# Prompt attention in a hybrid decoder layer: queries built a unit sooner, compressed scores on column quarters a unit later and transposed in two steps

## The chip, the cores and the metric

The kernel runs on one core of a Trainium2 chip. The metric is the device time of that core for one launch, in microseconds (us). Five engines work side by side, each through its own instructions in the order in which they are written: TensorE (PE; its weight loads are shown apart as PEld), VectorE (DVE), ScalarE (ACT), GpSimd (POOL) and SyncE (SP), which here issues transfers.

## The reference

One step of a decoder layer for 256 prompt tokens and 8 sample sequences of 8 tokens (320 token columns in all): a half FFN, a mixer of two branches (a Mamba-2 scan and a sparse attention with compressed, selected and window parts, 16 query heads on 4 key heads), and a second half FFN.

```python
def rmsnorm(x, g):
    xf = x.astype(jnp.float32)
    y = xf * lax.rsqrt(jnp.mean(xf * xf, axis=-1, keepdims=True) + EPS)
    return (y * g.astype(jnp.float32)).astype(x.dtype)
...
def masked_softmax(s, mask):
    s = jnp.where(mask, s.astype(jnp.float32), -jnp.inf)
    m = jnp.max(s, axis=-1, keepdims=True)
    m = jnp.where(jnp.isfinite(m), m, 0.0)
    e = jnp.exp(s - m)
    return e / jnp.maximum(jnp.sum(e, axis=-1, keepdims=True), 1e-30)
```

The part that the change touches is the prompt's attention. Its compressed branch scores each query against one key for every 32 tokens (8 for 256 tokens), and takes a masked softmax over them. Its values are weighted by these, by the selected and window scores, and by a gate for each head and branch.

## The kernel before

**Dense stream.** All large products (input projection, output projections, both FFNs) run through `dense` (L330 on). For each 128-row group of the contraction it issues three matmuls of 320 columns, which stand for one float32 product: high part by high part (L345), low by high (L346), high by low (L347). I call such three a *k-group*. SP streams the weights in blocks of 512 KB (L308). ACT makes each block's high part (`wh`, L317), and DVE its low part (`wl`, L326), so ACT, then DVE, work ahead of PE on every block.

**Side work.** After each k-group `dense` gives the scheduler a tick (`Sched`, L120 on). The scheduler advances generators, one of which is the attention: every `yield` ends one *step* of it. So a generator's instructions are spread between k-groups, and one step more of waiting moves everything that the generator issues by one step against the dense stream. `wait(n)` is n steps with nothing in them. The same projection feeds the convolution of the Mamba branch: ACT copies (`pr`, L1234), POOL makes the first tap (`cvo`, L1241), DVE three more (L1245), ACT a tanh (`cvt`, L1246), DVE the gated output (L1249, L1252).

**Prompt attention** (`prompt_attn`, L1255 on) has four chunks of 64 queries, eight units each, 32 units in all. POOL clears a buffer (L1267). `build` (L1281) writes a chunk's negated queries into it, in two POOL instructions. `cmp_a` computes the chunk's compressed scores: eight matmuls against 128 columns of queries (L1288), then a chain of small DVE and ACT operations (L1293 to L1303) that makes the softmax and applies the gate. `cmp_b` transposes half of the result on PE (L1310), and ACT copies it (L1311). For each unit there are the scores (PE L1317, DVE L1323, ACT L1326), a norm (DVE L1334, POOL L1337), transposes (PE L1349, ACT copy L1350) and values (PE L1366, with an ACT copy at a chunk's end, L1370).

**Another generator** runs ahead of it: `values_tok` (PE transposes L1035 and L1041, ACT copies), `new_keys` (key transposes, copied by DVE at L1127; PE L1053), and the sample tokens' compressed attention (PE L1212). Behind the attention the Mamba scan reads its states with transfers on SP (`h`, L1770), which stand in SP's one line with the weight blocks; PE uses them at L1819.

**PSUM banks** go by tag, round robin: three for the dense stream, two for `pt`, two for `sc`, one for `po`. A matmul into a bank waits until its last reader is done.

Of the kernel before, what the change touches and what calls it, by code (L numbers as in the profile page):

```python
# [191 lines left out]
def wait(n):  # L192
    for _ in range(n):
        yield
# [3 lines left out]
def step_kernel(ctx, tc, I, O):  # L198
    nc = tc.nc
    pe, v, a, g, sp = nc.tensor, nc.vector, nc.scalar, nc.gpsimd, nc.sync  # L200
# [10 lines left out]
    def bank(tag, shape=(128, 512)):  # L211
        bufs = dict(pd=3, sc=2, pt=2, po=1)[tag]
        t = ps.tile([128, 512], F32, tag=tag, bufs=bufs, name=f"ps_{tag}")[: shape[0], : int(np.prod(shape[1:]))]
        if len(shape) == 3:
            t = t.rearrange("p (a b) -> p a b", a=shape[1])
        elif len(shape) == 4:
            t = t.rearrange("p (a b c) -> p a b c", a=shape[1], b=shape[2])
        return t
# [4 lines left out]
    pt = cp.tile([1, 128], I32, name="pt")  # L223
# [16 lines left out]
    def flat(t):  # L240
        return t.rearrange("p a b -> p (a b)")
# [608 lines left out]
    kTp = pp.tile([128, 2, 8], F32, name="kTp")  # L850
# [17 lines left out]
    def bl(o, m, n):  # L868
        return st["blob"][:, o : o + m * n].rearrange("p (a b) -> p a b", a=m)
# [160 lines left out]

    def values_tok():
        for t in range(2):
            pv = bank("pt")
            for i in range(4):
                pe.transpose(pv[:, 128 * i : 128 * i + 128], vr[:, i, 128 * t : 128 * t + 128], ident)  # L1035
            a.copy(flat(vtp[:, t]), pv)
            yield
        pv = bank("pt", (128, 256))
        for br in range(2):
            for h2 in range(2):  # L1040
                pe.matmul(pv[64 * br : 64 * br + 64, 128 * h2 : 128 * h2 + 128], vr[:, 2 * br + h2, 256:], ident,  # L1041
                          start=True, stop=True)
        a.copy(vst, pv)
        yield
# [216 lines left out]
    def prompt_attn():  # L1261
# [3 lines left out]
        qbp = [bl(1024 * i, 8, 128) for i in range(2)]  # L1265
# [4 lines left out]
        def move():  # L1270
            if ready["prep"] and "OT" not in st:
                st["OT"] = hp_.tile([128, 8, NT], F32, tag="OT", name="OT")
            if moves and "OT" in st:
                t = moves.pop()
                a.copy(st["OT"][:, :, t], qn[:, :, t])


        def build(qc):
            for hp in range(2):
                r = slice(64 * hp, 64 * hp + 64)  # L1280
                g.tensor_scalar(qbp[qc % 2][r, :, 64 * hp : 64 * hp + 64], qn[r, 0:8, 64 * qc : 64 * qc + 64], -1.0, 0.0,  # L1281
                                op0=ALU.mult, op1=ALU.add)

        def cmp_a(qc):
            nb, k0 = 2 * (qc + 1), 192 - 64 * qc
            pc = bank("pt", (128, 8, 8))
            for u in range(8):
                pe.matmul(pc[:, u, :nb], qbp[qc % 2][:, u, :], kTp[:, u // 4, :nb], start=True, stop=True)  # L1288
            sc = pl.tile([128, 8, 8], F32, tag="psc", name="psc")
            m = pl.tile([128, 8], F32, tag="psm", name="psm")  # L1290
            s = sc[:, :, :nb]
            bcast = m.unsqueeze(2).to_broadcast([128, 8, nb])
            v.tensor_tensor(s, pc[:, :, :nb], pb[:, :, k0 + 31 :: 32], op=ALU.add)  # L1293
            v.tensor_reduce(out=m, in_=s, axis=AX.X, op=ALU.min)
            v.tensor_scalar(m, m, 1e20, None, op0=ALU.min)
            v.tensor_tensor(s, s, bcast, op=ALU.subtract)
            a.activation(s, s, AF.Exp, scale=-1.0)
            v.reduce_sum(m, s, axis=AX.X)
            v.tensor_scalar(m, m, 1e-30, None, op0=ALU.max)
            v.reciprocal(m, m)  # L1300
            gq = gtp[:, qc].rearrange("p (u r) -> p u r", r=3)
            v.tensor_tensor(m, m, gq[:, :, 0], op=ALU.mult)
            v.tensor_tensor(s, s, bcast, op=ALU.mult)  # L1303
            pend["c"] = sc

        def cmp_b(qc, q):
            nb, sc = 2 * (qc + 1), pend["c"]
            tps = bank("pt")
            for i in range(4):
                pe.transpose(tps[:nb, 128 * i : 128 * i + 128], sc[:, 4 * q + i, :nb], ident)  # L1310
            a.copy(flat(pcT[qc % 2][:nb, 4 * q : 4 * q + 4]), tps[:nb])  # L1311

        def scores(i):
            qc, u = divmod(i, 8)
            nk, k0 = 64 * (qc + 1), 192 - 64 * qc
            p = bank("sc", (128, 2, 256))
            pe.matmul(p[:, :, :nk], qbp[qc % 2][:, u, :], knp[:, :, u // 4, :nk], start=True, stop=True)  # L1317
            P = pl.tile([128, 2, 256], F32, tag="pS", bufs=4, name="pS")
            if nk % 128:
                g.memset(P[:, :, nk : nk + 64], 0.0)  # L1320
            m = pl.tile([128, 4], F32, tag="pm", bufs=6, name="pm")
            for br in range(2):
                v.tensor_tensor_reduce(out=P[:, br, :nk], in0=p[:, br, :nk], in1=pb[:, u, k0:256], op0=ALU.add,  # L1323
                                       op1=ALU.min, scale=1.0, scalar=3e38, accum_out=m[:, br : br + 1])
            for br in range(2):
                a.activation(P[:, br, :nk], P[:, br, :nk], AF.Exp, bias=m[:, br : br + 1], scale=-1.0,  # L1326
                             accum_out=m[:, 2 + br : 3 + br])
            pend["s", i] = P, m

        def norm(i):  # L1330
            qc, u = divmod(i, 8)
            nk = 64 * (qc + 1)
            P, m = pend["s", i]
            v.reciprocal(m[:, 2:4], m[:, 2:4])  # L1334
            for br in range(2):
                o = 3 * u + 1 + br
                g.tensor_scalar(P[:, br, :nk], P[:, br, :nk], m[:, 2 + br : 3 + br], gtp[:, qc, o : o + 1], op0=ALU.mult,  # L1337
                                op1=ALU.mult)


        def transposes(i):
            nt = (i // 8 + 2) // 2
            P = pend.pop(("s", i))[0]
            tps = bank("pt")
            pT = pl.tile([128, 4, 128], F32, tag="pT", bufs=2, name="pT")
            for k in range(nt):
                for br in range(2):
                    o = (k * 2 + br) * 128
                    pe.transpose(tps[:, o : o + 128], P[:, br, 128 * k : 128 * k + 128], ident)  # L1349
            a.copy(flat(pT[:, 0 : 2 * nt, :]), tps[:, 0 : 256 * nt])  # L1350
            pend["t", i] = pT

        def values(i):

            qc, u = divmod(i, 8)
            h2, nt = u // 4, (qc + 2) // 2
            pT = pend.pop(("t", i))
            if u == 0:
                pend["po"] = bank("po", (128, 8, 64))
            po = pend["po"]  # L1360
            parts = [(vtp[:, k, br, 128 * h2 : 128 * h2 + 128], pT[:, 2 * k + br]) for k in range(nt) for br in range(2)]
            parts.append((flat(vcp[:, 2 * h2 : 2 * h2 + 2, :]), pcT[qc % 2][:, u]))
            for j, (w, x_) in enumerate(parts):
                for hp in range(2):
                    h = slice(64 * hp, 64 * hp + 64)
                    pe.matmul(po[h, u, :], w[:, h], x_[:, h], start=j == 0, stop=j == len(parts) - 1)  # L1366
            if u == 7:

                o = st["OT"] if "OT" in st else qn
                a.copy(o[:, :, 64 * qc : 64 * qc + 64], po)  # L1370
                if o is qn:
                    moves.append(slice(64 * qc, 64 * qc + 64))

        build(0)
        yield from wait(2)
        cmp_a(0)
        yield from wait(4)
        cmp_b(0, 0)
        cmp_b(0, 1)
        for i in range(4):  # L1380
# [6 lines left out]
        for i in range(32):  # L1387
            qc, u = divmod(i, 8)
            if i + 3 < 32:
                norm(i + 3)  # L1390
            if i + 1 < 32:
                transposes(i + 1)
            if i + 4 < 32:
                scores(i + 4)
            yield
            values(i)
            move()
            if qc < 3:
                if u == 1:
                    build(qc + 1)  # L1400
                elif u == 2:
                    cmp_a(qc + 1)
                elif u == 4:
                    cmp_b(qc + 1, 0)
                    cmp_b(qc + 1, 1)
            yield
        pr_stack.close()
        yield from until("prep")
# [467 lines left out]
    def attention():  # L1876
        yield from chain(pace(3), prompt_attn(), pace(4), ssd(), pace(5), sample_attn(), pace(6), merge_prep())
# [54 lines left out]
    for i in range(4):  # L1932
# [5 lines left out]
        c, h2 = divmod(i, 2)  # L1938
# [281 lines left out]
```

## Time and profile before

| what | value |
|---|---|
| runs | 1324.02, 1332.32, 1332.83 us (median 1332.32) |
| profiled execution | 1327.57 us, of which the trace spans 1325.9 us |
| busy share of the span | PE 95%, PEld 87%, DVE 66%, ACT 45%, POOL 28% |
| mean granted clock of TensorE | 0.982 of full speed |

The trace is of one execution, and 1.67 us of its time lie outside the span. A busy share is an average over stages with different limits. The attention of the prompt lies between about 498 and 659 us of the span.

### The profile page before, as it was taken

The page shows a single profiled execution, that of the slowest core. Times are in us where ns is not written, and L with a number is a line of the kernel's source. Part 1 is how long each engine was busy: PE and PEld are TensorE (multiplying, and loading weights), DVE is VectorE, ACT ScalarE, POOL GpSimd, SP SyncE. Part 2 cuts the span into 40 slices and gives each one's busy share as a digit, 9 for nine tenths or more (in the row PEclk, how much of TensorE's full clock was granted, in tenths as well). Part 3 has the DMA queues.
Part 4 walks back from the last instruction along what each step waited for, and adds up shares of the span by engine and source line. Part 5 has one row for each costly group of instructions (what it writes and reads, how often), then busy time and mean ns, then how long its engine had stood idle before and what let it go on. Part 6 is the DMA issues. An engine that isn't in the chain of part 4 may idle for free.

```text
span 1325.9 us, 28576 instructions
## 1 busy us (share of the span) xinstructions
PE 1262.7 (95%) x10779; PEld 1149.6 (87%) x10779; DVE 877.8 (66%) x1872; ACT 590.7 (45%) x1149; POOL 372.7 (28%) x625
## 2 busy tenths in 40 slices
PE   8999999999999998889998898998989999999998
PEld 8899999999988888777896576776769999999998
DVE  5576666655576577975578687778667766666542
ACT  4344444454444334446664343456563343333322
POOL 2232321323100335655435353444420010000000
PEclk9899999999989999999999899999999999999999
DMA  8466665677653445511177775899973534444553
GB/s 278 153 210 216 209 200 190 219 227 216 212 163 125 142 138 206 191 66 63 49 223 244 220 222 174 315 357 313 343 274 115 178 130 146 156 146 157 152 162 92
DMA packets 98501, 251.67 MB, mean 190 GB/s; under 512 B 14649, under 2 KB 41274, under 8 KB 96410
## 3 DMA queue, kind: packets, MB, share of 16 engines
q1 hardware_dynamic: 81370, 198.24, 45.5%
q0 software_dynamic: 16992, 51.61, 11.7%
q8 instruction: 85, 1.39, 0.4%
q14 instruction: 54, 0.43, 0.1%
HBM read 235.07 MB, written 23.10 MB: 195 GB/s over the span
## 4 chain that ended last, share of the span: by engine, by line
PE 57%; DVE 17%; issue 12%; ACT 5%; DMA 4%; POOL 3%; SPq 1%; POOLq 1%; DVEq 0%; ACTq 0%
PE ps_pd L345 15%; PE ps_pd L346 13%; PE ps_pd L347 13%; DVE wl L326 4%; ACT wh L317 2%; DVE cvo L1245 2%; DMA out_ssmS<-h 2%; PE ps_sc L1478 2%; PE ps_po L1518 1%; PE ps_sc L713 1%; PE ps_sc L714 1%; PE ps_sc L723 1%; PE ps_pt L1504 1%; PE ps_po L1366 1%; PE ps_sc L1317 1%
## 5 line engine op out<-in xcount | busy, mean ns | idle before, releaser
L345 PE MATMUL ps_pd<-hh,wh 128*128 128x320 f32 x1320 | 440.7, 334 | 2.9 <-ACT hh L261 1.8
L326 DVE TENSOR_TENSOR wl<-wraw,wh 128x1024 fp32r<-128x1024 f32 (+1 forms) x245 | 305.4, 1248 | 184.9 <-ACT wh L317 179.4
L346 PE MATMUL ps_pd<-hl,wh 128*128 128x320 f32 x1320 | 413.4, 313 | 1.3 <-DVE hl L454 1.1
L347 PE MATMUL ps_pd<-hh,wl 128*128 128x320 f32 x1320 | 413.5, 313 | 1.1 <-DVE wl L326 1.1
L317 ACT CAST wh<-wraw 128x1024 fp32r<-128x1024 f32 (+1 forms) x245 | 252.2, 1031 | 139.8 <-PE ps_pd L346 100.7
L345 PEld LDWEIGHTS ps_pd<-hh,wh 128*128 128x128 f32 x1320 | 252.9, 192 | 22.0 <-issue 11.3
L346 PEld LDWEIGHTS ps_pd<-hl,wh 128*128 128x128 f32 x1320 | 253.4, 192 | 9.6 <-issue 4.8
L347 PEld LDWEIGHTS ps_pd<-hh,wl 128*128 128x128 f32 x1320 | 252.6, 191 | 1.6 <-DVE wl L326 1.6
L345 PE MATMUL ps_pd<-ah,wh 128*128 128x320 f32 x352 | 109.4, 311 | 0.0
L347 PE MATMUL ps_pd<-ah,wl 128*128 128x320 f32 x352 | 108.9, 309 | 0.0
L580 DVE TENSOR_TENSOR pgl<-pg,pgh 128x512 fp32r<-128x512 f32 x128 | 82.5, 685 | 29.7 <-ACT pgh L573 28.8
L346 PE MATMUL ps_pd<-al,wh 128*128 128x320 f32 x320 | 98.8, 309 | 0.0
L568 POOL DMA_DIRECT2D pg<-in_cache x136 | 74.2, 546 | 83.4 <-DVE pgl L580 42.3
L238 POOL TENSOR_SCALAR ah<-ff 128x320 fp32r<-128x320 f32 x44 | 20.1, 456 | 272.5 <-DVE ff L482 272.5
L573 ACT CAST pgh<-pg 128x512 fp32r<-128x512 f32 x128 | 72.7, 617 | 9.7 <-PE ps_sc L714 9.0
L477 ACT ACTIVATE sg<-sg 128x320 f32<-128x320 f32 x44 | 20.8, 472 | 125.7 <-DVE sg L476 125.7
L1431 POOL DMA_DIRECT2D KV<-in_cache x102 | 54.9, 539 | 76.4 <-PE ps_po L1518 43.2
L713 PE MATMUL ps_sc<-pgh,w1h 128*128 128x256 f32 x256 | 68.5, 288 | 1.0 <-ACT pgh L573 1.0
L714 PE MATMUL ps_sc<-pgh,w1l 128*128 128x256 f32 x256 | 68.3, 289 | 0.0
L345 PEld LDWEIGHTS ps_pd<-ah,wh 128*128 128x128 f32 x352 | 66.2, 188 | 0.4
L347 PEld LDWEIGHTS ps_pd<-ah,wl 128*128 128x128 f32 x352 | 66.1, 188 | 0.0
L346 PEld LDWEIGHTS ps_pd<-al,wh 128*128 128x128 f32 x320 | 60.2, 188 | 0.0
(476 smaller groups left out, 2207.9 us busy)
## 6 DMA issues: line engine op xcount, KB each, us to landing
wraw<-in_wproj SPq DMA_DIRECT2D x77, 512.0 KB
KV<-in_cache POOLq DMA_DIRECT2D x102, 256.0 KB, 6.1
wraw<-in_w1in SPq DMA_DIRECT2D x44, 512.0 KB
wraw<-in_w2in SPq DMA_DIRECT2D x44, 512.0 KB
pg<-in_cache POOLq DMA_DIRECT2D x136, 128.0 KB, 4.0
pg<-in_cache SPq DMA_DIRECT2D x120, 128.0 KB
wraw<-in_w1out SPq DMA_DIRECT2D x16, 512.0 KB
h<-in_ssm SPq DMA_DIRECT2D x32, 256.0 KB
```

The lines of the kernel that those rows point to most:

```text
L317: a.copy(h[:, :n], st["raw"][i][:, :n])
L326: v.tensor_tensor(l[:, :n], st["raw"].pop(i)[:, :n], st["hl"][i][0][:, :n], op=ALU.subtract)
L345: pe.matmul(out, wh[:, s], xh[:, kk, :], start=kk == 0, stop=False)
L346: pe.matmul(out, wh[:, s], xl[:, kk, :], start=False, stop=False)
L347: pe.matmul(out, wl[:, s], xh[:, kk, :], start=False, stop=kk == K - 1)
L568: e.dma_start(page(s, half)[:, i, :], I["cache"][ds(r, 1), :, 256 * c : 256 * c + 256].rearrange("o p f -> p (o f)"))
L573: a.copy(h[:, 8 * half : 8 * half + 8, :], page(s, half)[:, :, 64 * q : 64 * q + 64])
L580: v.tensor_tensor(l[:, 8 * half : 8 * half + 8, :], page(s, half)[:, :, 64 * q : 64 * q + 64], h[:, 8 * half : 8 * half + 8, :], op=ALU.su ...
L713: pe.matmul(ph, wh[:, j, :], h[:, :, j, :], start=q + j == 0, stop=False)
L714: pe.matmul(ph, wl[:, j, :], h[:, :, j, :], start=False, stop=False)
L1245: v.scalar_tensor_tensor(o, pr[:, k : k + 344], w(k), o, op0=ALU.mult, op1=ALU.add)
L1431: e.dma_start(t[:, j, :], I["cache"][ds(r, 1), :, 512:1024].rearrange("o p f -> p (o f)"))
```

## The change

There are four edits. First, the second of two banks in `values_tok` comes from the tag `sc` instead of `pt`. Second, each compressed-score matmul against 128 columns of queries becomes four, against 32 columns each, and each writes 32 output rows: 32 instructions for a chunk instead of 8. Third, at the start the wait ahead of the first `cmp_a` is four steps instead of two, and the one behind it three instead of four: seven steps instead of six before the first unit. Fourth, in the loop over units `build` of the next chunk comes at unit 0 (was 1), `cmp_a` at unit 3 (was 2), and the two halves of `cmp_b` at units 5 and 6 (were both at 4).

```diff
     def values_tok():
         for t in range(2):
-            pv = bank("pt")
+            pv = bank("sc" if t else "pt")
...
             for u in range(8):
-                pe.matmul(pc[:, u, :nb], qbp[qc % 2][:, u, :], kTp[:, u // 4, :nb], start=True, stop=True)
+                for c in range(4):
+                    o = slice(32 * c, 32 * c + 32)
+                    pe.matmul(pc[o, u, :nb], qbp[qc % 2][:, u, o], kTp[:, u // 4, :nb], start=True, stop=True)
...
         build(0)
-        yield from wait(2)
+        yield from wait(4)
         cmp_a(0)
-        yield from wait(4)
+        yield from wait(3)
         cmp_b(0, 0)
         cmp_b(0, 1)
...
             if qc < 3:
-                if u == 1:
+                if u == 0:
                     build(qc + 1)
-                elif u == 2:
+                elif u == 3:
                     cmp_a(qc + 1)
-                elif u == 4:
-                    cmp_b(qc + 1, 0)
-                    cmp_b(qc + 1, 1)
+                elif u in (5, 6):
+                    cmp_b(qc + 1, u - 5)
             yield
```

On PE, the compressed scores of the last chunk (`blob` is the queries' buffer, `pT` and `vtp` the transposed weights and the values), before:

```order
L1366 MATMUL ps_po<-pT,vtp 64x64 x8
L1366 MATMUL ps_po<-blob,vcp 64x64 x2
L1288 MATMUL ps_pt<-kTp,blob 128x8 x8
L345 MATMUL ps_pd<-hh,wh 128x320
L346 MATMUL ps_pd<-hl,wh 128x320
L347 MATMUL ps_pd<-hh,wl 128x320
L1349 MATMUL ps_pt<-con,pS 128x128 x4
```

and after:

```order
L1368 MATMUL ps_po<-pT,vtp 64x64 x8
L1368 MATMUL ps_po<-blob,vcp 64x64 x2
L1290 MATMUL ps_pt<-kTp,blob 32x8 x32
L345 MATMUL ps_pd<-hh,wh 128x320
L346 MATMUL ps_pd<-hl,wh 128x320
L347 MATMUL ps_pd<-hh,wl 128x320
L1351 MATMUL ps_pt<-con,pS 128x128 x4
```

The neighbours are the same, and 32 matmuls of 32 rows stand where 8 of 128 stood. Counted in k-groups from the start of the program, the four chunks' `cmp_a` stand behind the 738th, 775th, 818th and 845th before, and the 743rd, 783rd, 826th and 849th now; the scan starts behind the 883rd before and the 884th now.

On POOL, the queries of the second chunk (L1281; `pr`, `ncv` and `cvo` are the convolution's, `pS` the scores being normed), before:

```order
L238 TENSOR_SCALAR pr_4944<-scv 128x8x3
L238 TENSOR_SCALAR ncv<-pr_4944 128x3
L238 TENSOR_SCALAR ncv<-pr_4944 128x24
L1241 TENSOR_SCALAR cvo<-pr_4944,cwh 128x344
L1281 TENSOR_SCALAR blob<-qn 64x8x64 x2
L1337 TENSOR_SCALAR pS<-pS,pm,gtp 128x64 x2
L1320 MEMSET pS 128x2x64
```

and after:

```order
L1322 MEMSET pS 128x2x64
L1281 TENSOR_SCALAR blob<-qn 64x8x64 x2
L238 TENSOR_SCALAR pr_4944<-scv 128x8x3
L238 TENSOR_SCALAR ncv<-pr_4944 128x3
L238 TENSOR_SCALAR ncv<-pr_4944 128x24
L1241 TENSOR_SCALAR cvo<-pr_4944,cwh 128x344
L1339 TENSOR_SCALAR pS<-pS,pm,gtp 128x64 x2
```

The two instructions that write the queries have moved ahead of one convolution unit.

On SP, the scan's state loads (`h`), before:

```order
L1625 DMA abs<-ascr 64x8x64
L1625 DMA ab<-ascr 128x8x128
L1770 DMA h_8768<-in_ssm 128x512
L1770 DMA h_8775<-in_ssm 128x512
L1723 DMA out_ssmS<-h_8299 128x512
L308 DMA wraw<-in_wproj 128x1024
L1770 DMA h_8793<-in_ssm 128x512
```

and after:

```order
L1626 DMA abs<-ascr 64x8x64
L1626 DMA ab<-ascr 128x8x128
L308 DMA wraw<-in_wproj 128x1024
L1771 DMA h_8874<-in_ssm 128x512
L1771 DMA h_8881<-in_ssm 128x512
L1724 DMA out_ssmS<-h_8402 128x512
L1771 DMA h_8895<-in_ssm 128x512
```

One weight block (L308) now stands ahead of two state loads that it stood behind. The same happens in one other batch of the scan's loads, and in one later batch the other way round.

## Rows read from the trace of the kernel before

**Rows 1.** The head of the page, and the busy time of each engine with its share of the span.

```profile
span 1325.9 us, 28576 instructions
PE 1262.7 (95%) x10779; PEld 1149.6 (87%) x10779; DVE 877.8 (66%) x1872; ACT 590.7 (45%) x1149; POOL 372.7 (28%) x625
```

**Rows 2.** Windows: a stretch of the span (us), its length, the busy time and count of PE, PEld, DVE, ACT and POOL, the granted clock, the share of the DMA engines and their GB/s.

```profile
486.90:571.00 84.10, 67.89 (x704) 61.40 (x701) 69.40 (x178) 37.13 (x115) 51.96 (x90) 0.94 0.50 183
...
600.00:626.00 26.00, 25.98 (x263) 21.48 (x262) 16.60 (x64) 18.12 (x55) 14.83 (x34) 1.00 0.13 42
```

**Rows 3.** The chain of waits from 480 to 640 us: start (us), length (us), the engine, tile and line on the chain.

```profile
497.98 3.46 POOL blob L1267
...
502.27 0.79 POOL blob L1281
503.10 1.96 PE ps_pt L1288 x16
...
507.20 1.14 DVE wl L326
...
551.22 0.50 ACT cvt L1246
...
583.65 1.89 PE ps_pt L1288 x16
...
616.55 1.88 PE ps_pt L1288 x16
```

**Rows 4.** Waits of DVE, ACT and POOL from 486.9 to 571 us, by what they waited for: total us, times, longest. The first row is the only one of the three engines' lists in which PE is waited for.

```profile
DVE psc L1293 <- PE ps_pt L1288: 0.5, 1, 0.5
...
DVE wl L326 <- ACT wh L317: 6.9, 6, 1.6
...
ACT cvt L1246 <- DVE cvo L1245: 22.7, 6, 5.7
...
POOL ncv L238 <- ACT pr L1234: 12.1, 7, 4.8
```

**Rows 5.** Waits of PE from 486.9 to 626 us, in the same columns.

```profile
PE ps_po L1366 <- ACT qn L1370: 3.6, 1, 3.6
PE ps_pt L1288 <- POOL blob L1281: 2.9, 2, 2.0
PE ps_pt L1310 <- ACT pT L1350: 2.9, 1, 2.9
PE ps_pt L1035 <- DVE kTp L1127: 2.6, 1, 2.6
...
PE ps_pt L1349 <- ACT blob L1311: 0.7, 1, 0.7
```

**Rows 6.** The timeline of the four compressed-score groups: start, length (us), engine, line, operation, tiles, shapes, count of passes (two for each float32 matmul), and the idle time before with what ended it.

```profile
503.10 1.95 PE L1288 MATMUL ps_pt<-kTp,blob 128*128 128x2 f32 x16 [0.88 <-POOL blob L1281]
...
537.88 1.95 PE L1288 MATMUL ps_pt<-kTp,blob 128*128 128x4 f32 x16 [2.03 <-POOL blob L1281]
...
583.58 1.95 PE L1288 MATMUL ps_pt<-kTp,blob 128*128 128x6 f32 x16
...
616.48 1.95 PE L1288 MATMUL ps_pt<-kTp,blob 128*128 128x8 f32 x16
```

**Rows 7.** The timeline of two other groups of 64 small passes, against 32 columns of weights (L1212, which also fills four quarters of output rows in turn) and against 64 columns (L1053).

```profile
593.15 1.10 PE L1212 MATMUL ps_sc<-kcv,cpT 128*32 128x64 f32 x64
...
496.91 2.04 PE L1053 MATMUL ps_sc<-ksm,qbs 128*64 128x8 f32 x64
```

**Rows 8.** Windows of 3.4 us, PE alone: stretch, length, busy time and count, granted clock, DMA share, GB/s.

```profile
494.20:497.60 3.40, 3.40 (x36) 0.72 0.38 145
...
504.40:507.80 3.40, 3.40 (x22) 0.79 0.04 7
507.80:511.20 3.40, 3.40 (x19) 0.71 0.86 328
541.80:545.20 3.40, 3.40 (x26) 0.69 0.02 5
...
585.40:588.80 3.40, 3.40 (x27) 1.00 0.00 0
```

**Rows 9.** The timeline around the second bank of `values_tok`: the copy that frees it, its transposes, and the next user of the tag.

```profile
491.18 0.16 DVE L1127 COPY kTp<-ps_pt 128x16 f32<-128x16 f32 x1
491.40 0.66 PE L1035 MATMUL ps_pt<-con,vr 128*128 128x128 f32 x4 [2.58 <-DVE kTp L1127]
492.97 1.13 PE L1041 MATMUL ps_pt<-con,vr 128*64 128x128 f32 x8
```

**Rows 10.** The timeline behind the first compressed scores: ACT's high part and DVE's low part of the block in work, and one score operation of a unit on DVE from further on.

```profile
504.26 1.06 ACT L317 CAST wh<-wraw 128x1024 fp32r<-128x1024 f32 x1
507.12 1.22 DVE L326 TENSOR_TENSOR wl<-wraw,wh 128x1024 fp32r<-128x1024 f32 x1
...
532.84 0.20 DVE L1323 CUSTOM_DVE_ANT_0 pS<-ps_sc,pb 128x64 f32<-128x64 f32 x1
```

**Rows 11.** The timeline of the second chunk's queries on POOL.

```profile
535.66 2.17 POOL L1281 TENSOR_SCALAR blob<-qn 64x512 f32<-64x512 f32 x2
```

**Rows 12.** PE's waits for the scan's states from 680 to 1000 us, and a window of that stage (columns as in rows 2).

```profile
PE ps_po L1819 <- DMA h<-in_ssm: 8.9, 5, 2.9
...
720.00:760.00 40.00, 34.54 (x203) 24.47 (x200) 26.57 (x43) 12.39 (x27) 18.37 (x14) 0.87 0.68 216
```

## The prediction

> **What bounds the kernel now.** I read the head of the page first: PE is busy for 1262.7 of 1325.9 us [rows 1]. That is an average, so I next read windows over the prompt's attention, where the edits lie. It falls into two stages [rows 2]. From 486.9 to 571 us PE is busy for 67.89 of 84.10 us and DVE for 69.40. In a stage behind it, 600 to 626 us, PE is busy for 25.98 of 26.00 us, and no other engine is near that.
>
> The chain of waits says who sets the pace in each [rows 3]. In the first stage its pieces are POOL's clearing of the buffer, POOL's queries, DVE's low parts and ACT's tanh; of the edited lines only the first compressed scores (1.96 us at 503.10) are on it on PE's side. At 537.88, where the second chunk's scores ran [rows 6], the chain is elsewhere. In the second stage the third and the fourth chunk's scores are on it (1.89 us at 583.65, 1.88 us at 616.55).
>
> The waits say the same from the other side. Between 486.9 and 571 us DVE waited for PE once, for 0.5 us; ACT and POOL never did [rows 4]. Their long waits are for each other: ACT's tanh for DVE's convolution, 22.7 us; POOL's `ncv` for ACT's copy, 12.1 us; DVE's low part for ACT's high part, 6.9 us. That loop (copy, first tap, three taps, tanh, and on the way the split of the next block) paces the stage. PE's own waits there [rows 5] are then mostly the time that it has to spare: a wait removed comes back as a wait for the next low part.
>
> **The change part by part.**
>
> *Column quarters.* Before, a chunk's scores are 16 passes in 1.95 us [rows 6]; now they are 64 passes of a quarter of the columns. The nearest row has the same form, 64 passes against 32 columns, four quarters of output rows in turn: 1.10 us. The other end is 64 passes against 64 columns, 2.04 us [rows 7]. So a group becomes 0.85 us shorter (1.95 - 1.10) or, at the other end, 0.09 us longer; the four together give 3.4 us back, or cost 0.4. I take 0.85, as the row of 1.10 us has the same column count and the same turn of output rows. Only the third and the fourth chunk lie where PE sets the end, so 2 x 0.85 = **1.7 us** are on the path (the bounds are 3.4 saved and 0.4 lost).
>
> Those 64 passes at L1212 took 17 ns each (1.10 us by 64) [rows 7]. [...]
>
> *The first compressed scores, two steps later.* They left a wait of 0.88 us for POOL's queries and 1.95 us of work [rows 6], on the chain [rows 3]. Behind them the low part started at 507.12, though ACT's high part had ended at 505.32 (504.26 + 1.06) [rows 10]; DVE did the softmax chain of that chunk in between. Now the low part, and the convolution's taps, stand ahead of that chain. So up to 1.8 us could go, but the chain's operations come behind the taps all the same, on an engine with 69.40 us of work in 84.10. Between 0 and 1.8 I take **0.5 us**, near the lower end since only the order of DVE's work changes.
>
> *Queries sooner, scores later, in the loop.* The waits of PE for POOL's queries (2.9 us in two) should go, and those at the transposes in two steps with them (2.9 and 0.7 us) [rows 5], as three units instead of one now lie between writing and use, and one copy of ACT instead of two behind each transposed half. The 2.03 us at the second chunk are off the chain, and so are the transposes' 2.9 us, behind which the chain stands at ACT's tanh (551.22) [rows 3]. I cost both at **nothing**: DVE's work is their cover, and were it gone, 2.0 + 2.9 + 0.7 = 5.6 us would be the gain. What is late next is the low part of the next block. The two POOL instructions (2.17 us) [rows 11] now stand ahead of a convolution unit's first tap. POOL has 12.1 us of waiting for ACT's copies in this stage [rows 4], in seven waits, mean 1.7 us, and that hides them; if one fell on a late copy, up to 2.2 us would be lost. I take nothing.
>
> *The second bank of `values_tok`.* The wait of 2.58 us for the key copy goes to the next user of the tag, the transposes at L1041, which now wait for the same copy (it ends at 491.34) [rows 9]. Of 2.58 us some 1.6 can go: that next group started 1.57 us behind the waiting one (492.97 - 491.40), and it can at most come so much sooner. At 491 us the chain is on POOL and DVE, and POOL's buffer clearing (497.98) [rows 3] is not behind PE. I take **nothing** (bounds 0 and 1.6 saved).
>
> *The clock.* [...] One fall covers two windows, at 0.79 and 0.71, and takes 3.4 x (0.21 + 0.29) = 1.7 us of work from them. [...]
>
> *One step more at the start.* The attention's operations move one step against the dense stream, which takes about four DVE operations of a unit at 0.20 us each [rows 10], **0.8 us**, out of the stage that DVE paces into the one where DVE has time. The bounds are 0 and 2, and the other way 0.5 lost where the tail behind the attention comes later. In the scan, one weight block moves ahead of state loads in two batches and behind in one; costed at nothing, since PE's waits for the states, 8.9 us in five [rows 12], may grow or shrink with it. This is the second rival.
>
> The sum is 1.7 + 0.5 + 0.8 = 3.0 us less. Against the profiled execution's 1327.57 us that is 1324.6. This execution is 4.75 us below the median shown (1332.32); the four executions, this one and the three runs, average 1329.2. As the forecast is compared with runs and not with this execution, I put it at 1329.2 - 3.0, rounded: **1326 us**.
>
> **The rivals.**
>
> *All of PE's gains reach the end.* Then the quarters give 3.4, the queries' waits 2.9, the transposes' 2.9 + 0.7, `values_tok` 1.6 and the clock 5.1: 16.6 us, so 1327.6 - 16.6 = **1311 us**. For it speaks that PE is busy for 95% of the span and that a shorter wait on PE frees weight buffers sooner. Against it speak the chain and that nobody waited for PE [rows 3, 4]. Chance 0.13.
>
> *The states come late.* Where a 512 KB block goes ahead of the states, they land later by its passage: at 216 GB/s [rows 12] 2.4 us, in two batches 4.8. Each such stall of PE can draw a stretch at a lower clock as in [rows 8], 1.7 us each, 3.4 together. Slower by 8.2 us, **1336 us**. It decides once PE's waits for the states exceed the 8.9 us of now by more than the 3.0 us won. Against it: a later batch moves the other way round, and the weight block that now goes first is itself one that the dense stream needs. Chance 0.12.
>
> *The quarters save nothing*, or weight loads don't overlap: 2.04 us for a group instead of 1.95, all four on the path, 0.4 us lost, and the rest a wash: **1328 to 1330 us**, no change. It decides if a small pass lasts as at L1053 (2.04 us by 64, 32 ns) and not as at L1212. [...] Chance 0.10.
>
> **How the numbers follow.** The forecast has the remaining 0.65. About 1%, 13 us, is what a measurement of this kernel can tell from no change. The forecast's own range goes from 3.4 + 1.8 + 2 = 7.2 us saved to 0.4 + 2.2 + 0.5 = 3.1 lost, on a base of 1324.6 to 1332 that the runs spread over: 1319 to 1335. For 8 in 10 the range also goes three quarters of the way from 1324.6 to the first rival, and takes in the second: **1314 to 1337 us**. Faster by over 1% is the first rival nearly whole, 0.11; slower by over 1% needs the second rival and a loss at POOL together, 0.06; within 1% stays 0.83.
>
> **What would show it.** In the profile of the changed kernel: four groups of 64 passes at 1.1 us in place of 1.95; no wait of PE for POOL's queries at any chunk; the wait at the transposes below 1 us; and, between 487 and 571 us, waits of PE for the low part in place of those that went, with this stage's length within 2 us of 84.1. The third and the fourth chunk's scores should still be on the chain, shorter. The forecast is wrong if that stage becomes shorter by much of what PE no longer waits (then the first rival holds), or if the waits for the states exceed 12 us (then the second).

## The result, and the profile after

The change made the kernel slower. Its median is 1337.03 us over 14 runs (1333.65 to 1343.95), against 1331.51 us for the kernel before in the same comparison. The recorded ratio of the two is 1.0064, with a 95% interval of 1.0048 to 1.0080. That is 8.5 us, less than the 1% that I had named as telling apart, but clear of this measurement's noise. The two medians alone differ by 5.5 us (1.0041), so the size is less sure than the sign. The forecast of 1326 us had the sign wrong, and the range ended at 1337.

The head of the page of the changed kernel, answering to [rows 1]:

```profile
span 1337.8 us, 28951 instructions
PE 1266.5 (95%) x10971; PEld 1151.7 (86%) x10971; DVE 878.0 (66%) x1872; ACT 589.4 (44%) x1149; POOL 373.9 (28%) x625
```

The work is the same: DVE, ACT and POOL are busy for as long as before, within 1.3 us, and the span is 11.9 us longer. That is more than the change costs by its runs: the traced execution of the changed kernel (1339.42 us) lies above its median, that of before (1327.57 us) below. So the question is where PE waits or runs slowly. To find the place I followed one operation that every weight block has, DVE's low part (L326), and read its start in both traces at the same block. First the kernel before, at the 131st and the 141st block, then the changed kernel at the same two:

```profile
774.10 1.21 DVE L326 TENSOR_TENSOR wl<-wraw,wh 128x1024 fp32r<-128x1024 f32 x1
...
849.19 1.22 DVE L326 TENSOR_TENSOR wl<-wraw,wh 128x1024 fp32r<-128x1024 f32 x1
```

```profile
770.16 1.21 DVE L326 TENSOR_TENSOR wl<-wraw,wh 128x1024 fp32r<-128x1024 f32 x1
...
855.22 1.22 DVE L326 TENSOR_TENSOR wl<-wraw,wh 128x1024 fp32r<-128x1024 f32 x1
```

Up to the first of them the changed kernel is 3.9 us ahead. (At the 90th block, ahead of all edits, the traces of the seventeen kernels of this document stand up to 8 us apart. So only lengths of stretches are compared here.) Over the next ten blocks, all in the Mamba scan, it falls 10.0 us back (85.06 us where 75.09 were needed), and 3 us are lost in each of two stretches further on; what loses these is not shown. The attention, which the edits are about, is not where the time went: between the starts of the 96th and the 121st block (498.00 to 690.27 us before, 496.55 to 685.50 us after) it is 3.3 us shorter.

PE's waits of the changed kernel between 480 and 660 us, answering to [rows 5]:

```profile
PE ps_pt L1351 <- POOL pS L1339: 7.1, 3, 6.3
PE ps_pt L1312 <- DVE psc L1305: 4.9, 1, 4.9
PE ps_pt L1351 <- ACT pT L1352: 3.3, 1, 3.3
PE ps_pt L1312 <- ACT blob L1313: 2.4, 2, 1.8
...
PE ps_pt L1041 <- DVE kTp L1127: 1.3, 1, 1.3
```

The waits for POOL's queries are gone, and others have taken their place: 4.9 us for DVE's softmax of the first chunk, 7.1 us for the norm. The quarters themselves did more than forecast. Here are the timeline of the first group and the weight loads of all four, in place of the 1.95 us and 128 columns of [rows 6]; the other three groups took 0.71 to 0.72 us:

```profile
501.48 0.85 PE L1290 MATMUL ps_pt<-kTp,blob 128*32 128x2 f32 x64
...
L1290 PEld LDWEIGHTS ps_pt<-kTp,blob x256: 106/110/113, 501.5 to 620.0; 128*32 128x32 f32 x128
```

PE's waits of the changed kernel from 760 to 900 us:

```profile
PE ps_pt L1848 <- DVE ys L1836: 6.6, 1, 6.6
PE ps_sc L1825 <- DVE h L1827: 2.9, 3, 2.2
PE ps_po L1820 <- DMA h<-in_ssm: 2.1, 1, 2.1
```

The first row is new. It is the transpose of `ys`, the part of the sample tokens' output that comes from their states. What it waits for is read from two timelines and the chain of waits. SP's timeline, the kernel before and then the changed one:

```profile
820.13 6.70 SPq L1723 DMA_DIRECT2D out_ssmS<-h  x4
826.88 0.42 SPq L1723 DMA_DIRECT2D out_ssmP<-St  x1
829.76 1.62 SPq L1431 DMA_DIRECT2D KV<-in_cache  x2
831.87 0.34 SPq L308 DMA_DIRECT2D wraw<-in_wproj  x1
```

```profile
818.86 6.66 SPq L1724 DMA_DIRECT2D out_ssmS<-h  x4
830.91 0.34 SPq L308 DMA_DIRECT2D wraw<-in_wproj  x1
831.30 0.42 SPq L1724 DMA_DIRECT2D out_ssmP<-St  x1
```

POOL's, the kernel before and then the changed one (`[...]` is the idle time before a row, and what ended it):

```profile
822.96 2.07 POOL L1821 TENSOR_TENSOR h<-h,cdb 128x512 f32<-128x512 f32 x2 [6.09 <-issue]
830.25 1.16 POOL L1431 DMA_DIRECT2D KV<-in_cache  x2 [5.21 <-DVE zth L2002]
831.42 2.36 POOL L1821 TENSOR_TENSOR h<-h,cdb 128x512 f32<-128x512 f32 x2
```

```profile
823.37 2.09 POOL L1822 TENSOR_TENSOR h<-h,cdb 128x512 f32<-128x512 f32 x2 [7.53 <-DMA out_ssmS<-h]
836.15 1.16 POOL L1432 DMA_DIRECT2D KV<-in_cache  x2 [10.70 <-DMA out_ssmP<-St]
837.33 2.08 POOL L1822 TENSOR_TENSOR h<-h,cdb 128x512 f32<-128x512 f32 x2
```

And the chain of waits of the changed kernel through the same stretch (start, length, what):

```profile
829.67 1.23 DVE wl L326
830.91 0.34 SPq L308
...
831.30 4.16 DMA out_ssmP<-St
...
838.34 1.07 POOL h L1822
839.44 0.69 DVE h L1827
840.12 0.60 DVE ys L1836
...
841.57 1.22 DVE wl L326
```

Read from the top: the weight block's load (L308) waits until DVE has used up a buffer: it goes at 830.91 us, where the low part ends (829.67 + 1.23). In the changed order it stands in SP's line ahead of the last store of the prompt's state (`out_ssmP`). The data of the store were ready at 821.37 us (DVE, L1711), and nothing else stood ahead on SP from 825.52 us on. But the store waits with the block until 831.30 instead of going at 826.88. POOL's next instruction, a load of the sample attention's keys (`KV`), waits for that store (the program closes the pool that holds the stored tile just ahead of these loads). Behind it on POOL stands the scaling of the states, `h`, which DVE needs for `ys`, which PE needs. PE stands still for 6.65 us.

The low parts of the 137th and the 138th block enclose this wait: they start at 829.67 and 841.57 us here, and at 830.63 and 835.95 before. So 6.6 of the 10.0 us arise in this one place. The other 3 build up ahead of it; kernels with SP's order of before, further down, are up to 3.0 us longer there too.

### The profile page after: what moved, and what is told of

Read it like the earlier page. It is cut to its first block, busy times and chain, and to the rows that moved or that the text cites. A ratio compares the mean times of both kernels' runs of the same rounds, so it can differ in the third digit from the quotient of the medians.

```text
span 1337.8 us, 28951 instructions
## 1 busy us (share of the span) xinstructions
PE 1266.5 (95%) x10971; PEld 1151.7 (86%) x10971; DVE 878.0 (66%) x1872; ACT 589.4 (44%) x1149; POOL 373.9 (28%) x625
## 5 line engine op out<-in xcount | busy, mean ns | idle before, releaser
L326 DVE TENSOR_TENSOR wl<-wraw,wh 128x1024 fp32r<-128x1024 f32 (+1 forms) x245 | 304.5, 1244 | 184.8 <-ACT wh L317 180.4
```

The lines of the kernel that those rows point to most:

```text
L326: v.tensor_tensor(l[:, :n], st["raw"].pop(i)[:, :n], st["hl"][i][0][:, :n], op=ALU.subtract)
```

## The experiments

Theory Q: the one step more at the start moves the scan against the dense stream, weight blocks come to stand ahead of the scan's transfers on SP, and the scan pays. The rivals: the edits inside the attention cost it (A); it is the granted clock, falling at places that no order decides (C). Every ratio below is to the kernel before, timed together with it; the bracket is its 95% interval, and a number of us is the ratio's distance from 1 times the median of before.

**The step alone, and the change without it.**

```diff
-        yield from wait(4)
+        yield from wait(5)
         cmp_b(0, 0)
```

> The kernel before with one thing changed: the second wait at the start of the prompt attention is 5 steps instead of 4, seven in all, as in the change; no quarters, no moved build, scores or transposes. Its order on SP is that of the change. Theory Q (the one step puts weight blocks ahead of stores and state loads in SP's line, and the scan pays for it): slower than before by 8 to 14 us, ratio 1.006 to 1.010, with a wait of PE of 4 us or more at the transposes of ys (L1847). Rival A (the edits inside the attention cost the time, for instance by falls of the clock): no difference from before, ratio 0.998 to 1.002. Rival C (falls of the granted clock at places that no order decides): anything between 0.998 and 1.008, with no long wait behind the last store of the prompt's state.

Measured: 1.0134 [1.0105, 1.0163], 17.8 us slower, more than expected. Its one new long wait from 760 to 900 us:

```profile
PE ps_pt L1847 <- DVE ys L1835: 6.2, 1, 6.2
```

```diff
         cmp_a(0)
-        yield from wait(3)
+        yield from wait(2)
```

> The change with the second wait at the start 2 steps instead of 3, six in all, as before; all else of the change kept. Its order on SP is that of the kernel before. Theory Q: faster than before by the attention's gain alone, 2 to 5 us, ratio 0.996 to 0.999, and no wait of PE over 2 us at the transposes of ys. Rival A: as slow as the change, ratio 1.004 to 1.008. Rival C: between 0.997 and 1.008.

Measured: 0.9977 [0.9951, 1.0004], 3.1 us faster or no difference. The step alone makes a worse kernel than the whole change, and the change without the step loses nothing: rival A falls, and C with it, as the same fall would have to follow the step in one kernel after the other. The two do not add up, though: 17.8 less 3.1 would be 14.7 us, and the change measured 8.5. What makes up the difference stays open. In the attention of the kernel without the step PE waits longer for DVE's softmax than in the change (9.5 us in two, where there are 4.9 in one), without harm:

```profile
PE ps_pt L1312 <- DVE psc L1305: 5.7, 1, 5.7
PE ps_pt L1351 <- DVE psc L1295: 3.8, 1, 3.8
```

**Which of the two that the step moves, attention or scan.**

```diff
             yield
+        yield
         pr_stack.close()
```

> The kernel before with one empty step behind the last unit of the prompt attention, so that the attention itself stands as before and the scan one step later; the order on SP is that of the change. Theory Q (the scan's place in the dense stream costs the time): nearly the whole cost of the step at the start, slower than before by 10 to 18 us, ratio 1.008 to 1.014, with a wait of PE of 4 us or more at the transposes of ys. Rival A2 (most of that cost is the later attention): 0 to 5 us, ratio 1.000 to 1.004.

Measured: 1.0107 [1.0082, 1.0132], 14.2 us slower, with the same wait, of 6.8 us:

```profile
PE ps_pt L1848 <- DVE ys L1836: 6.8, 1, 6.8
```

The counterpart has seven steps at the start and leaves out the last empty step behind the units:

```diff
-        yield from wait(4)
+        yield from wait(5)
...
-            yield
+            if i < 31:
+                yield
         pr_stack.close()
```

> The kernel before with seven steps at the start of the attention, and the empty step behind its last unit left out: the attention stands one step later, the scan where it stood; the order on SP is that of the kernel before. Theory Q: within 3 us of before, ratio 0.998 to 1.002. Rival A2: slower by 8 us or more, ratio above 1.006.

Measured: 1.0033 [1.0014, 1.0051], 4.4 us slower. The two parts, 14.2 and 4.4, come to 18.6, close to the 17.8 of the step at the start. So the scan carries most of it, and the attention's later place a part that neither theory had expected. From the 101st to the 111th block that part shows (stretch, length, busy time and count of PE, PEld, DVE, ACT, POOL, granted clock, DMA), the kernel before and then this one:

```profile
535.71:624.45 88.74, 76.92 (x719) 66.35 (x714) 67.98 (x201) 45.68 (x144) 54.00 (x103) 0.96 0.27 96
```

```profile
534.64:628.30 93.66, 83.09 (x740) 71.41 (x740) 68.27 (x201) 46.64 (x149) 51.26 (x106) 0.89 0.26 91
```

The stretch is 4.9 us longer at the same work, and the granted clock is 0.89 where it was 0.96; PE is busy for 6 us more. Whether the clock or the waits around it come first wasn't tried.

The same cut on the change, its scan put back and its attention left a step later:

```diff
-            yield
+            if i < 31:
+                yield
         pr_stack.close()
```

> The change in full, with the empty step behind the attention's last unit left out, so that the scan stands where it stood before; the order on SP is that of the kernel before. Theory Q: as the change without its extra step, faster than before by 2 to 5 us, ratio 0.996 to 0.999. Rival A2: still slower than before, ratio above 1.003.

Measured: 1.0019 [1.0001, 1.0038], 2.5 us slower, between the two expectations. By the middle values two thirds of the change's loss (6.0 of 8.5 us) are gone with the scan's place alone, and against the 0.9977 with six steps the attention's later place costs 0.4% here too. The traces place a part of that: from the 101st to the 106th block the four kernels with the attention of the change (this one, the change itself and two more below) need 45.9 to 46.1 us, and the four with its moves in the loop and six steps 42.8. In every trace the order on SP is as expected: the step alone and the step behind have the order of the change, and the kernel without the step, the one with seven steps and this one have that of before.

**Is it SP's order, or the later place on PE and DVE?** SP's order can be put back without moving the scan: the loads of 28 weight blocks are issued behind the fifth k-group of a block instead of the third.

```diff
             st["hl"][i][1] = l
-            w_load()
+            if not 122 <= i < 150:
+                w_load()
...
+                if k == 4 and 122 <= st["split"] - 1 < 150:
+                    w_load()
                 if (kk + 1) % cut == 0:
```

> The change, with the loads of 28 weight blocks of the scan's stage (numbers 122 to 149) issued behind the fifth k-group of the block in work instead of the third. So SP's order is again that of the kernel before, but for two blocks that stand one or two places later still; on PE, DVE, ACT and POOL the scan keeps the change's later place. Theory Q (SP's order is what the later scan pays for): 6 to 9 us of the change's loss come back, ratio to before 0.999 to 1.002, no wait of 4 us at the transposes of ys. Rival P (the later place of the scan's operations on PE and DVE is what costs): as the change, 1.005 to 1.008.

Measured: 0.9987 [0.9969, 1.0005]. The whole loss came back, with the scan as late as in the change. By the middle values that is more than the scan's share: the attention stands late here too, and its 0.4% is not seen in this kernel. On SP the store now goes right behind the stores of the states:

```profile
816.91 0.33 SPq L1727 DMA_DIRECT2D out_ssmS<-h  x1
817.30 0.70 SPq L1727 DMA_DIRECT2D out_ssmP<-St  x1
820.20 0.91 SPq L1435 DMA_DIRECT2D KV<-in_cache  x2
```

and `ys` is not among PE's waits from 760 to 900 us, which begin with:

```profile
PE ps_pt L399 <- DVE ncol L404: 3.3, 1, 3.3
PE ps_sc L1828 <- DVE h L1830: 2.9, 3, 2.2
PE ps_po L1823 <- DMA h<-in_ssm: 1.7, 1, 1.7
```

Two more kernels ask whether the later loads are a gain of their own. The same edit on the kernel before:

> The kernel before with nothing but the 28 weight loads of the scan's stage behind the fifth k-group instead of the third; the scan stands where it stood, so that SP's order is now a new one, in which weight blocks stand behind transfers of the scan that they stood ahead of. If the later loads are a gain by themselves, and the change's recovery came from that: ratio 0.990 to 0.995. Theory Q (what counts is where the blocks stand among the scan's transfers): no such gain, 0.998 to 1.012.

Measured: 0.9986 [0.9968, 1.0004], no gain that can be told. And the same edit with the empty step behind the last unit:

> The kernel before with the empty step behind the last unit (which alone gave a ratio of 1.0107) and the 28 loads behind the fifth k-group. Theory Q in its barest form: SP's order is back but for two blocks, so the loss goes, ratio 0.997 to 1.002, and no wait of PE of 4 us at the transposes of ys. Rival P (the later place on PE and DVE costs): above 1.006.

Measured: 0.9982 [0.9960, 1.0003], against 1.0107 with the step alone. Between these two kernels only the place of the weight loads differs, and it is worth 1.2%. Theory Q stands for the scan, and the scan's later place on PE and DVE costs nothing that can be told. The traces say the same: between the 137th and the 138th block the change, the step alone and the step behind lose 6.6, 6.6 and 6.7 us against the kernel before, and no other kernel of this document more than 0.9.

**That one store, or several transfers.** The change, with the last store one step sooner:

```diff
                     load_ecb(q + 1)
+                if i == 7:
+                    store("outS")
                 yield
                 store("outS")
```

> The change, with the last store of the prompt's state (out_ssmP) issued one step sooner, so that it stands ahead of the weight block that the change had put in front of it; nothing else moves on SP. Theory Q in its narrow form (that one store behind that one weight block holds POOL's KV loads, the scaling of the states behind them on POOL, and so PE at the transposes of ys): 6 to 9 us of the loss come back, ratio to before 0.999 to 1.002. Theory Q in its wide form (several transfers moved, each costs a part): 1 to 4 us come back, ratio 1.003 to 1.005. Rival A and rival C: as the change, 1.005 to 1.008.

Measured: 1.0029 [1.0009, 1.0048]; by the middle values 4.7 of 8.5 us came back, between the narrow and the wide form. As 2.5 us stayed lost with the scan's place put back altogether, that is most of the scan's share. In the trace the stretch from the 131st to the 141st block is 8.6 us shorter than in the change. The store now goes out ahead of two stores of states, and the wait at `ys` is gone:

```profile
818.13 0.33 SPq L1724 DMA_DIRECT2D out_ssmP<-St  x1
818.52 4.31 SPq L1724 DMA_DIRECT2D out_ssmS<-h  x2
```

The other way round, the kernel before with that store one step later, behind a weight block and two stores of states:

```diff
                 yield
+                if i == 7:
+                    yield
                 store("outS")
```

> The kernel before, with one more step of waiting ahead of the last store of the prompt's state, so that a weight block and two stores of states stand in front of it, as one block does in the change; everything up to that point is as before. Narrow form of theory Q: slower than before by 5 to 9 us, ratio 1.004 to 1.007, with a wait of PE of 4 us or more at the transposes of ys. Wide form: 0 to 3 us, ratio 1.000 to 1.002. Rivals A and C: no difference, 0.998 to 1.002.

Measured: 1.0049 [1.0022, 1.0077], 6.5 us slower, a time within the narrow form's. But its runs spread from 1322.02 to 1341.05 us, and the profiled one (1329.58 us) shows another chain, without a wait at `ys`. Two rows are POOL's, the last is PE's:

```profile
820.10 4.11 POOL L1823 TENSOR_TENSOR h<-h,cdb 128x512 f32<-128x512 f32 x4 [6.10 <-issue]
835.97 1.16 POOL L1431 DMA_DIRECT2D KV<-in_cache  x2 [11.76 <-DMA out_ssmP<-St]
...
847.12 1.58 PE L1478 MATMUL ps_sc<-KV,qbs 64*32 64x512 f32 x14 [2.23 <-DMA KV<-in_cache]
```

The added step moves the `KV` loads as well, and on POOL all four scalings of the states now stand ahead of them. So the late store, issued at 830.42 us, holds the `KV` loads and not `ys`, and PE waits for the keys themselves; 5.8 us are lost there, between the 141st and the 142nd block. The run shows that this store can be dear when it is late, but it does not test the chain of the change; for that chain the kernel with the store sooner speaks. The other transfers that moved were not taken apart.

**The edits without the step.** The quarters alone:

> The kernel before with the column quarters alone. In the change's profile a group of 64 passes took 0.85 us instead of 1.95, 1.1 us less. If only the third and the fourth chunk's groups are on the path: 2.2 us faster, ratio 0.998. If all four are: 4.4 us, ratio 0.9967. If none is, or what PE gains comes back as a wait for DVE: 1.000. No order moves on SP.

Measured: 1.0001 [0.9978, 1.0025]. The gain of the third and the fourth chunk (2.2 us, or 2.5 with the 0.72 us that their groups took) lies within the interval's reach, that of all four (4.4 or more) doesn't. The moves in the loop alone:

> The kernel before with the moves in the loop alone (queries at unit 0, scores at unit 3, transposes at units 5 and 6); six steps at the start, no quarters. If the stalls of PE for POOL's queries and at the transposes are mostly spare time, as forecast: within 2 us of before, ratio 0.9985 to 1.0015. If they are on the path: 4 to 6 us faster, ratio 0.9955 to 0.997.

Measured: 1.0007 [0.9995, 1.0020]: the waits for the queries and at the transposes were spare time of PE. The bank of `values_tok` and the longer wait ahead of the first scores were not run alone.

**One step less, and what could beat both kernels.** Five steps at the start of the kernel before (3 for 4):

> The kernel before with five steps at the start instead of six, so that attention and scan both stand one step sooner; on SP five weight blocks stand behind transfers of the scan that they stood ahead of. Theory Q, if sooner is better all the way: faster by 3 to 10 us, ratio 0.992 to 0.998. Theory Q, if only the one place counts where a weight block stood ahead of the last store of the prompt's state: no difference, 0.998 to 1.002, as this store stands free of it before too. If each place is a matter of luck: anything up to 1.01.

Measured: 1.0096 [1.0063, 1.0129], 12.8 us slower; sooner is no better. Here PE's longest wait between 700 and 900 us is another, for the states:

```profile
PE ps_po L1819 <- DMA h<-in_ssm: 10.4, 4, 5.5
```

Its trace is 20.4 us longer than that of before; 6.0 of these arise between the 101st and the 106th block, in the attention, and 6.9 between the 141st and the 151st. What does it stays open. The change with six steps and the store sooner, too:

> The change with six steps at the start and the last store of the prompt's state issued one step sooner: both remedies together, the version that should beat the kernel before. Expected: as the change with six steps, ratio 0.995 to 0.999, since that store stands ahead of the weight block there already; a gain of more than 3 us beyond that would say that POOL's KV loads still wait for it.

Measured: 1.0002 [0.9985, 1.0019], slower than expected, and no gain over the six steps alone. The change with six steps, an empty step behind the last unit, and the 28 loads later:

> The change with six steps at the start (the attention as early as before), one empty step behind its last unit (the scan as late as in the change) and the 28 weight loads behind the fifth k-group: SP's order as in the kernel before but for two blocks. If the gains add (six steps instead of seven gave 0.0042 in ratio with the scan's place kept, the later loads 0.0077 on the change): ratio 0.993 to 0.997, faster than both kernels. If they don't: 0.997 to 1.001.

Measured: 0.9972 [0.9955, 0.9989], 3.7 us faster than the kernel before and, by the two ratios, 0.9% faster than the change. That is where the expectation has the gains not adding up. It is the one version of fifteen whose interval leaves 1 out on the fast side, and the two medians differ by only 1.9 us, so it is little to build on.

## Why the prediction was wrong

*The scan.* The step that failed is this one: "In the scan, one weight block moves ahead of state loads in two batches and behind in one; costed at nothing". It cost about 10 us in the trace of the changed kernel (75.09 us became 85.06 between the two blocks), of which 6.6 are the one wait at `ys`; by the runs it is 6.0 us in the change and 14.2 by itself. I had looked at the loads of the states, as their wait was the row that the trace of before showed [rows 12]. That wait did not grow (7.1 us from 680 to 1000 us, where it had been 8.9). What grew was a wait with no row before, behind a store on the same line of SP, past which the weight block had moved as well. The order of the instructions showed it ahead of the run: weight block, then the last `out_ssmP`, where the block had come behind. I counted the block's moves past loads and never its moves past stores, nor asked who on POOL waits for a store.

The second rival said 1336 us, and 1337.03 was measured, but by another mechanism than it named; that the two lie so close is chance. Its form was right, a transfer late behind a weight block and PE standing still; its place and its price (2.4 us for the block's passage at [rows 12]) were not. Here the block didn't cost its passage, but the time until DVE freed its buffer: SP stood still from 825.52 to 830.91 us for it, the store went 4.4 us later than before, and POOL's `KV` load 5.9 us later (836.15 for 830.25).

*One step more at the start* was to save 0.8 us. This term failed as well: in the kernel before the attention's part of it costs 4.4 us. The clock and the waits between the 101st and the 111th block go with it, and which of them is the cause stays open. What the attention's later place costs in the change itself is not settled: 0.4% with the scan put back, nothing to be seen with the loads later.

*The first compressed scores* were sized about right, at 0.5 us. The low part behind them came 1.8 us sooner (7.35 us from the 96th block to the 97th, where it had been 9.12). At the 101st block 1.6 us of it were left in the trace of the change, and 0.5 in that of the change with six steps.

*The quarters.* Sized at 0.85 us saved for a group, they saved 1.10 in the first (0.85 us long) and 1.23 in the others (0.72). A pass took 13 and 11 ns, and each of these groups' weight loads 110 ns. The 64 loads of the first group would take 7.0 us one after the other and were through in 0.76, so they ran side by side, and the third rival's 2.04 us for a group is out. On the whole time the gain is too small to tell.

*Queries, scores and transposes at nothing* was right, and for the reason given in the main: the waits came back as others, and the moves alone gave 1.0007. But they came back as waits for DVE's softmax and for POOL's norm; a wait for the next low part, which was to be the sign, is not among them. The stage's length kept to its sign (84.91 us between the 94th and the 105th block, 83.96 before). That the wait at the transposes would fall below 1 us was wrong: it is 4.9 us for the first chunk, as the softmax on DVE now stands behind the convolution.

*The bank of `values_tok`* did as forecast: the wait is 1.3 us at the next user, where about 1.0 was expected.

*The clock.* The 5.1 us that the first rival's sum has for the clock are a term that no run shows. The runs showed in its place that the clock did not stay up where the queries' stalls went. In the attention and in the scan the changed kernel has, among others, these stretches at half speed, beside [rows 8]:

```profile
509.30:516.10 6.80, 5.19 (x23) 0.50 0.63 233
543.40:553.70 10.30, 5.92 (x30) 0.50 0.43 154
567.30:570.70 3.40, 3.12 (x11) 0.51 0.02 5
837.00:843.80 6.80, 2.93 (x12) 0.50 0.95 294
850.60:857.50 6.90, 6.90 (x36) 0.51 0.52 199
```

The first three lie in the attention, 20.5 us together; before, there were four of 3.4 us at 0.50 between 490 and 600 us, 13.6 together. The fourth stretch lies on the wait at `ys`; in the trace of before the clock is 1.00 from 800 to 900 us. The last stretch slows PE for 6.9 us at the 140th block; it is not shown to come from the wait.

*The attention's gain* came close to the sum, in part by luck. Without the term of the step the sum has 2.2 us, and the change without its step measured 3.1, in an interval from 6.5 faster to 0.5 slower; the quarters and the moves by themselves gave nothing that can be told. The 3.3 us of the trace are with the step, and in the runs the same attention with the scan put back lost 2.5 us.

*The range.* Its lower end for the forecast, 1319, doesn't follow from its terms: 7.2 us off the stated base of 1324.6 would be 1317, and that base has the 3.0 us of gain taken off already. The result lay at the other end, so this changes nothing.

## What to carry to other kernels

Where a scheduler interleaves work by steps, a step added in one place shifts all that follows, and the price may fall due far from the edit: compare the order on every queue to the end of the program, stores as well as loads. In SP's line a block that waited for a buffer held the store behind it (until 831.30 us, where it had gone at 826.88), so a prefetch that is not yet possible should stand behind a store that somebody waits for. Taking waits from an engine that is not the bound of its stage saved nothing here (1.0007).

## What the runs showed of the hardware that was not expected

Groups of 64 passes with two to eight columns streamed against 32-column quarters of the weights took 0.85 us once and 0.72 us three times, where 16 passes against 128 columns took 1.95: four times the instructions in less than half of the time. And a shift of one step of the scheduler in either direction, with the same work, made this kernel about 1% slower (1.0134 and 1.0096), more than the quarters (1.0001) or the moves in the loop (1.0007) changed it by themselves.
